# A decoder trunk on one core: four modulation vectors moved from TensorE to VectorE, low halves of the first mixer's weights no longer made ahead, and a planner with other durations

## The chip, the cores and the metric

The kernel runs on one core of a Trainium2 chip. The metric is the device time of one execution in microseconds, as the median of several runs. TensorE (PE) does the matrix products and transposes, VectorE (DVE) and ScalarE (ACT) the elementwise work, GpSimd (POOL) a few small operations. SyncE (SP) issues every transfer, in order, on one queue.

## What is computed

Two layers, each made of a SwiGLU feed-forward block, a token mixer and a second feed-forward block, on 256 tokens of width 1024 in float32. A conditioning vector gives nine modulation vectors per layer: a shift, a scale and a gate for each of the three sub-layers. Cut to what matters here:

```python
cond = silu(c)                                   # 1 x 1024
for l in range(2):
    mod = cond @ ada_w[l] + ada_b[l]             # 9 vectors of 1024
    sh1, sc1, gt1, sh2, sc2, gt2, sh3, sc3, gt3 = split(mod, 9)
    f1 = swiglu(x * (1 + sc1) + sh1, w1, w3, w2)             # F = 2816
    x = layer_norm(2**0.5 * x + 0.5 * gt1 * f1)
    m = token_mixer(x * (1 + sc2) + sh2)         # w_in 1024x2560, w_out 1024x1024
    x = layer_norm(2**0.5 * x + gt2 * m)
    f2 = swiglu(x * (1 + sc3) + sh3, v1, v3, v2)
    x = layer_norm(2**0.5 * x + 0.5 * gt3 * f2)
```

The mixer has three parts side by side: a gated linear recurrence, chunked retention, and a diagonal state-space model ("S5") whose output is `y = Re(C x)`, a complex product taken as sums of real ones.

## The kernel before

**Products in three terms.** Every large product is made from float32 operands split in a high half, rounded to fp32r, and a low half, the rest: three fp32r products for one (`mm3`, tiles `xTh`, `xTl` for the activations, `g_slot` for the hidden units, `wh_slot`, `wl_slot` for the weights). A weight block of 128x2048 (1 MB) arrives in a `raw_slot` (3 of them). ScalarE casts each half of it to `wh_slot`, VectorE subtracts to give `wl_slot` (8 of each, 128x1024). `Piece.convert` (line 805) does that. A block that is needed later can be split ahead: `ahead` and `split_ahead` (lines 844 to 858) load it, make its halves and store only the low halves in DRAM (`gtdl...`). When the block is used, its raw form is loaded again and cast again, and the low halves come by a transfer instead of VectorE's subtraction. Before the change this is done for the four blocks of `mix_w_out` of both layers and for six of the ten blocks of layer 1's `mix_w_in`.

**Modulation vectors, two ways.** `ada_matmul` (line 955) leaves a vector to TensorE: 8 chunks of `ada_w` (128x1024, 512 KB each) in `s_slot` tiles meet the condition repeated over 32 columns (`condrep`), 32 plain float32 products of 32x256 for a vector, in two fused groups of 16. `ada_group` (line 903) leaves four vectors to VectorE and ScalarE: 32 chunks hold rows of all four at once; half of them are multiplied by the condition and added by one VectorE instruction (`SCALAR_TENSOR_TENSOR`), the other half are scaled by ScalarE and added by VectorE (`TENSOR_TENSOR` 128x1024), and at the end TensorE transposes the sum and VectorE reduces it. Before, layer 0's vectors 2 to 7 go the first way and ten others the second. Vectors 0 and 1 have their own start. Vector 2 is the gate of the first sub-layer; 3 and 4 are shift and scale of the first mixer; 5 is its gate.

**Order.** Nothing of the order on the engines is written by hand. The program records all operations (`Scheduler.add`, line 325), each with a duration from `cost` (line 411). A list scheduler (`run`, line 496) lays them out in eight rounds with priorities from the round before (`place_late`), picks buffers as well, and keeps the round with the shortest planned span; `emit` writes the instructions in planned order. So any change of a duration or of the work can move instructions and buffers anywhere. The program text sets only what may stand where: `Background` items (modulation, parameters, low halves made ahead) are recorded between the units of a feed-forward block.

**S5 output.** `y_part` (line 1547) multiplies the scanned states by tables on VectorE, and TensorE sums the result over the states (32-column products with `CT`, four to a fused group). For the first half of the states (`u == 0`) VectorE first adds or subtracts the two products, so that TensorE has two groups; for the second half TensorE takes all four.

Profile lines all read L694, the line of `emit` from which every instruction is issued; instructions are told apart by their tiles.

Of the kernel before, what the change touches and what calls it, by code (L numbers as in the profile page):

```python
# [14 lines left out]
ALU = mybir.AluOpType  # L15
PSUM = bass.MemoryType.PSUM
# [126 lines left out]
class Op:  # L143
    __slots__ = ("i", "eng", "calls", "dur", "deps", "succ", "tiles", "banks", "func", "prio", "start", "end",
                 "alts", "pref", "pdur", "nbytes", "outname")
# [108 lines left out]
class Scheduler:  # L254
# [70 lines left out]
    def add(self, eng, m, real, a, k, alts=()):  # L325
# [21 lines left out]
        fs = 1  # L347
# [14 lines left out]
        for x, w in accs:  # L362
# [38 lines left out]
            self.hist[nm] = keep  # L401
        d, nb = op.dur, op.nbytes
        c = self.cost(eng, m, a, k, out, ins, nel, fs, scal, psum, op)
        if not first and out.shape[0] == 32:
            c = 27
        op.dur, op.nbytes = d + c, nb + op.nbytes
        op.pref, op.pdur = op.eng, op.dur
        for i, n, r in alts:
            op.alts[i] = (r, self.cost(i, n, a, k, out, ins, nel, fs, scal, psum, op))

    def cost(self, eng, m, a, k, out, ins, n, fs, scal, psum, op):
        if eng == E_SPQ:
            nb = 4
            for x in list(out.shape):
                nb *= x
            run = min(nb // (x_runs(out)), nb // x_runs(ins[0]))
            op.nbytes = nb * (0.94 if run >= 4096 else 1) if run >= 512 else max(2 * nb, nb // run * 157)
            src = ins[0].ap_ if isinstance(ins[0], VT) else ins[0]
            return 635 if "DRAM" not in str(src.space) or len(src.shape) != len(out.shape) else 460
        if eng == E_PE:  # L420
            if m == "transpose":
                op.nbytes = fs * ins[0].shape[0] / 128
                return 109.5
            cols = fs
            op.nbytes = fs * (1 if "float32r" in str(ins[0].dtype) else 4) * ins[0].shape[0] / 128
            if "float32r" in str(ins[0].dtype):
                return cols * 0.4246 + 8.6
            return max(cols, 128) * 4 * 0.4167 + 5
# [21 lines left out]
        if m == "tensor_copy":  # L450
            return 100 + 3.4 * n
        ops = str(k.get("op", k.get("op0", "")))
        if "pow" in ops:
            return 1075 + 68 * n
# [41 lines left out]
    def run(self, span, slack):  # L496
# [23 lines left out]
        info = self.tile_info  # L520

# [52 lines left out]
        while done < n:  # L574
# [41 lines left out]
            d = op.dur  # L616
            if op.func is not None and op.func:
                if cur_set is None or op.func not in cur_set:
                    d += 1280
                    cur_set = next(fs for fs in ACT_SETS if op.func in fs)  # L620
# [12 lines left out]
            if e == E_SPQ:  # L633
                efree[e] = s + d
                st = max(dma_free, s + 1060)
                dma_free = st + op.nbytes / 360
                op.end = dma_free + 1000
            else:
                op.end = s + d
                efree[e] = op.end  # L640
            for b in op.banks:
                bank_last.setdefault(b, {})[e] = op.end
# [61 lines left out]
def trunk_kernel(ctx: ExitStack, tc: tile.TileContext, a: dict, cst: bass.AP, out: bass.AP):  # L704
# [715 lines left out]
    def mixer(l, P, nxt, last_features, bg):  # L1420
# [126 lines left out]
        def y_part(u, ch):  # L1547
# [11 lines left out]
            for n, tabs in enumerate(((tcv, tsv), (tsv, tcv))):  # L1559
                p = [t2([128, 4, 128], f"pr{l}{ch}{u}{n}{i}") for i in range(2)]  # L1560
                for i, tab in enumerate(tabs):
                    VG.tensor_tensor(p[i], v[u][i][:, ch], tab[:, js, :], op=ALU.mult)
                    if u:
                        y_mm((0, 1)[i] if n == 0 else 2, p[i], n + i == 0, n + i == 2)
                if u == 0:
                    GV.tensor_tensor(p[0], p[0], p[1], op=ALU.add if n else ALU.subtract)
                    y_mm(2 * n, p[0], n == 0, n == 1)
# [368 lines left out]
    with tc.manual_schedule():  # L1936
# [17 lines left out]
        for l in range(L):  # L1954
            mp = mix_params(l, Ps[l])
            if l == 0:
# [5 lines left out]
                items = adam((0, 2), (0, 3), (0, 4), (0, 5))  # L1962
                extra = dict(enumerate([param_start] + param_steps()))
                extra.update({7: mp[0], 9: mp[1], 10: mp[2], 11: mp[3], 13: mp[4], 14: mp[5]})
                bg = Background(merge(attach(items, extra), ahead(0, [], (0, 256, 512, 768))), 5)
                late = Background(adam((0, 6), (0, 7)), 3)
            else:
                items = ada([(1, 5), (1, 6), (1, 7), (1, 8)])
                bg = Background(merge(attach(items, {2: mp[0], 4: mp[1], 6: mp[2], 8: mp[3], 10: mp[4], 12: mp[5]}),
                                      ahead(1, all_in[4:], (0, 256, 512, 768))), 7)  # L1970
# [35 lines left out]
```

## Time and profile before

| | |
|---|---|
| median of 3 runs | 1055.18 us (1053.9 to 1064.11) |
| profiled execution | 1052.99 us, of it 1051.2 us from first to last instruction |
| granted TensorE clock, mean | 0.99 |
| PE busy | 1007.4 us (96%) |
| PE weight loads busy | 893.4 us (85%) |
| DVE busy | 822.4 us (78%) |
| ACT busy | 572.3 us (54%) |
| moved by DMA | 304.94 MB, mean 290 GB/s |

A busy share is a mean over stages with different limits, so the rows below give it by stage too. Matmuls are pipelined: a row's duration runs past the start of the next one, and what a matmul costs PE is the distance from one start to the next. The feed-forward block of layer 0 runs to about 226 us, its mixer to about 361, the second block to about 533; layer 1 follows with bounds at about 737 and 858.

### The profile page before, as it was taken

How to read it: one execution, taken by the hardware profiler on the slowest of the kernel's cores; microseconds unless marked ns; L12 is line 12 of the kernel's file. 1: busy time of each engine (PE TensorE's matmuls, PEld its weight loads, DVE VectorE, ACT ScalarE, POOL GpSimd, SP SyncE). 2: the span in 40 equal slices, each digit the busy share in tenths (PEclk: the TensorE clock that was granted, in tenths of full speed). 3: DMA queues.
4: the chain of work that ended last, by engine and by line, in shares of the span. 5: the costliest groups of instructions: out<-in, count | busy, mean ns of one | idle time of the engine just before them, and what ended most of it. 6: DMA issues, size and time to landing. Idle time of an engine off the chain costs nothing.

```text
span 1051.2 us, 17641 instructions
## 1 busy us (share of the span) xinstructions
PE 1007.4 (96%) x7061; PEld 893.4 (85%) x7061; DVE 822.4 (78%) x1276; ACT 572.3 (54%) x737; POOL 27.9 (3%) x46
## 2 busy tenths in 40 slices
PE   5999999999988999999999999999999899999996
PEld 3788888888976789999987989999898779999995
DVE  3676675669998999999889999666989788554555
ACT  3565564334478666655547565555447755444440
POOL 0000000000001000000000000000000100000000
PEclk9999999999999999999999999999999999999999
DMA  9999989985679789999967999998478736555521
GB/s 362 404 339 354 355 333 362 378 319 192 216 250 351 252 284 388 400 373 344 355 253 265 337 385 366 355 360 315 163 289 360 301 123 237 176 186 201 188 93 40
DMA packets 70002, 304.94 MB, mean 290 GB/s; under 512 B 15520, under 2 KB 18080, under 8 KB 47904
## 3 DMA queue, kind: packets, MB, share of 16 engines
q1 hardware_dynamic: 69920, 303.82, 78.1%
q8 instruction: 55, 0.90, 0.3%
q14 instruction: 27, 0.22, 0.1%
HBM read 286.46 MB, written 15.75 MB: 287 GB/s over the span
## 4 chain that ended last, share of the span: by engine, by line
PE 79%; DVE 11%; DMA 6%; ACT 1%; issue 1%; SPq 0%; DVEq 0%; ACTq 0%
PE r_slot L694 79%; DVE s_slot L694 5%; DMA raw_slot<-in_pack_dram 5%; DVE wl_slot L694 3%; DVE x_res L694 1%; DMA s_slot<-in_ada_w_dram 1%; DVE ti_slot L694 1%; ACT wh_slot L694 1%; DMA g_slot<-g_slot 1%; SPq L694 0%; DVE xTl L694 0%; ACT s_slot L694 0%; DVE xTh L694 0%; DVE g_slot L694 0%; ACT L694 0%
## 5 line engine op out<-in xcount | busy, mean ns | idle before, releaser
L694 ACT CAST wh_slot<-raw_slot 128x1024 fp32r<-128x1024 f32 x348 | 355.9, 1049 | 274.6 <-PE r_slot L694 128.4
L694 DVE TENSOR_TENSOR wl_slot<-raw_slot,wh_slot 128x1024 fp32r<-128x1024 f32 x320 | 384.0, 1219 | 145.1 <-ACT wh_slot L694 136.7
L694 PE MATMUL r_slot<-xTh,wh_slot 128*128 128x256 f32 x1216 | 341.3, 281 | 0.0
L694 PE MATMUL r_slot<-xTh,wl_slot 128*128 128x256 f32 x1216 | 341.0, 281 | 0.0
L694 PE MATMUL r_slot<-xTl,wh_slot 128*128 128x256 f32 x1216 | 340.5, 280 | 0.0
L694 PEld LDWEIGHTS r_slot<-xTh,wl_slot 128*128 128x128 f32 x1216 | 231.7, 191 | 1.6 <-issue 1.6
L694 PEld LDWEIGHTS r_slot<-xTh,wh_slot 128*128 128x128 f32 x1216 | 229.1, 188 | 2.0 <-issue 0.8
L694 PEld LDWEIGHTS r_slot<-xTl,wh_slot 128*128 128x128 f32 x1216 | 229.0, 188 | 1.2
L694 PE MATMUL r_slot<-wh_slot,g_slot 128*128 128x512 f32 x704 | 224.7, 392 | 0.5 <-DVE g_slot L694 0.5
L694 PEld LDWEIGHTS r_slot<-wh_slot,g_slot 128*128 128x128 f32 x704 | 131.8, 188 | 27.4 <-DVE g_slot L694 0.9
L694 PE MATMUL r_slot<-wh_slot,xTh 128*128 128x512 f32 (+1 forms) x416 | 146.0, 352 | 5.8 <-DVE xTh L694 3.9
L694 PE MATMUL r_slot<-wh_slot,xTl 128*128 128x512 f32 (+1 forms) x416 | 144.0, 349 | 2.7 <-DVE xTl L694 2.7
L694 PE MATMUL r_slot<-wl_slot,xTh 128*128 128x512 f32 (+1 forms) x416 | 143.7, 347 | 0.5 <-DVE wl_slot L694 0.5
L694 PE MATMUL r_slot<-wl_slot,g_slot 128*128 128x512 f32 x352 | 137.5, 391 | 0.0
L694 DVE TENSOR_TENSOR s_slot<-s_slot,s_slot 128x256 f32<-128x256 f32 (+10 forms) x168 | 109.6, 676 | 6.8 <-ACT s_slot L694 4.3
L694 PEld LDWEIGHTS r_slot<-wh_slot,xTh 128*128 128x128 f32 x416 | 79.2, 191 | 18.4 <-DVE xTh L694 5.4
L694 PEld LDWEIGHTS r_slot<-wh_slot,xTl 128*128 128x128 f32 x416 | 79.3, 191 | 17.6 <-DVE xTl L694 4.4
L694 DVE TENSOR_TENSOR s_slot<-r_slot,s_slot 128x512 f32<-128x512 f32 x100 | 67.8, 683 | 28.4 <-PE r_slot L694 28.1
L694 PEld LDWEIGHTS r_slot<-wl_slot,xTh 128*128 128x128 f32 x416 | 79.3, 191 | 10.1 <-DVE wl_slot L694 0.7
L694 PEld LDWEIGHTS r_slot<-wl_slot,g_slot 128*128 128x128 f32 x352 | 66.1, 188 | 12.4 <-issue 0.4
L694 ACT ACTIVATE s_slot<-s_slot,cond 128x1024 f32<-128x1024 f32 x40 | 46.1, 1152 | 36.2 <-DMA s_slot<-in_ada_w_dram 36.1
L694 DVE SCALAR_TENSOR_TENSOR s_slot<-s_slot,cond,s_slot 128x1024 f32<-128x1024 f32 x37 | 47.3, 1278 | 4.5 <-DMA s_slot<-in_ada_w_dram 4.3
(123 smaller groups left out, 685.9 us busy)
## 6 DMA issues: line engine op xcount, KB each, us to landing
raw_slot<-in_pack_dram SPq DMA_DIRECT2D x172, 1024.0 KB
s_slot<-in_ada_w_dram SPq DMA_DIRECT2D x128, 512.0 KB
s_slot<-in_pack_dram SPq DMA_DIRECT2D x16, 512.0 KB
tdlmix_w_out<-wl_slot SPq DMA_DIRECT2D x12, 512.0 KB
wl_slot<-tdlmix_w_out SPq DMA_DIRECT2D x12, 512.0 KB
s_slot<-gtd SPq DMA_DIRECT2D x6, 512.0 KB
s_slot<-in_ln_g_dram SPq DMA_DIRECT2D x6, 512.0 KB
s_slot<-in_ln_b_dram SPq DMA_DIRECT2D x6, 512.0 KB
```

What stands on the lines that cost most here:

```text
L694: real(*[self.place(v) for v in a], **{n: self.place(v) for n, v in k.items()})
```

## The change

Six things are edited. (1) The planner's durations: float32 products of 32 rows cost more, small ones less; GpSimd's copies and powers cost less; a long transfer counts 0.97 of its bytes, not 0.94. (2) A new function `port` marks operations that use the read port shared by VectorE and GpSimd, and the planner lets a GpSimd operation wait for the end of a VectorE operation that is so marked. (3) Layer 0's vectors 2 to 5 go through `ada_group`, one group of four, not four times through `ada_matmul`. (4) No low halves are made ahead for layer 0's `mix_w_out`. (5) For layer 1 the blocks of `mix_w_in` that are split ahead go from six to three; its `mix_w_out` stays as it is. (6) In `y_part` TensorE takes all four products for both halves of the states, and VectorE's additions and subtractions there are gone.

```diff
         d, nb = op.dur, op.nbytes
         c = self.cost(eng, m, a, k, out, ins, nel, fs, scal, psum, op)
         if not first and out.shape[0] == 32:
-            c = 27
+            c = 27 if (len(op.calls) - 1) % 4 else 1.695 * fs
...
+    def port(self, eng, m, out, ins):
+
+        if eng == E_POOL:
+            return 3 if ins else 0
+        if eng != E_DVE:
+            return 0
+        psum = ["PSUM" in str((x.ap_ if isinstance(x, VT) else x).space) for x in [out] + ins]
+        if m in ("tensor_tensor", "tensor_tensor_scan", "scalar_tensor_tensor"):
+            return 0 if psum[1] or psum[-1] else 1
+        return 1 if m in ("tensor_scalar", "tensor_copy") and not psum[0] and not psum[1] else 0
...
-            op.nbytes = nb * (0.94 if run >= 4096 else 1) if run >= 512 else max(2 * nb, nb // run * 157)
+            op.nbytes = nb * (0.97 if run >= 4096 else 1) if run >= 512 else max(2 * nb, nb // run * 157)
...
-            return max(cols, 128) * 4 * 0.4167 + 5
+            return max(cols, 64) * 4 * 0.4167 + (65 if out.shape[0] == 32 else 5)
...
         if "pow" in ops:
-            return 1075 + 68 * n
+            return 394 + 156 * n
...
+            if op.port == 3 and s < held:
+                d = held - s + d - 140
...
+                if e == E_DVE and op.port:
+                    held = op.end
...
-                    if u:
-                        y_mm((0, 1)[i] if n == 0 else 2, p[i], n + i == 0, n + i == 2)
-                if u == 0:
-                    GV.tensor_tensor(p[0], p[0], p[1], op=ALU.add if n else ALU.subtract)
-                    y_mm(2 * n, p[0], n == 0, n == 1)
+                    y_mm((0, 1)[i] if n == 0 else 2, p[i], n + i == 0, n + i == 2)
...
-                items = adam((0, 2), (0, 3), (0, 4), (0, 5))
+                items = ada([(0, 2), (0, 3), (0, 4), (0, 5)])
...
-                bg = Background(merge(attach(items, extra), ahead(0, [], (0, 256, 512, 768))), 5)
+                bg = Background(merge(attach(items, extra), ahead(0, [], ())), 5)
...
-                                      ahead(1, all_in[4:], (0, 256, 512, 768))), 7)
+                                      ahead(1, all_in[7:], (0, 256, 512, 768))), 7)
```

In the built programs TensorE loses 128 of its 192 `condrep` products of 32x256 and gains 32 of `CT`. VectorE gains 15 `SCALAR_TENSOR_TENSOR` and 16 `TENSOR_TENSOR` of 128x1024, one `TENSOR_SCALAR` and two reductions, and loses eight `TENSOR_TENSOR` of 128x512; its count of low halves stays at 320. ScalarE loses 14 casts of weights and 4 copies and gains 16 scalings. SP loses 7 loads of raw blocks, 14 stores and 14 loads of low halves.

TensorE, in the first feed-forward block of layer 0, before: one fused group of a modulation vector (`condrep`, each row four products) between products of the up and down weights.

```order
L694 MATMUL r_slot_131<-wl_slot_80,g_slot_102 128x512
L694 MATMUL r_slot_124<-s_slot_92,condrep 32x256 x4
L694 MATMUL r_slot_124<-s_slot_93,condrep 32x256 x4
L694 MATMUL r_slot_124<-s_slot_83,condrep 32x256 x4
L694 MATMUL r_slot_124<-s_slot_84,condrep 32x256 x4
L694 MATMUL r_slot_126<-xTh,wl_slot_76 128x256
L694 MATMUL r_slot_131<-wh_slot_73,g_slot_103 128x512
```

VectorE, in the same block, of the change: the same vectors as multiply-adds on `cond` and additions of 128x1024, between low halves (`wl_slot`) and parameter work (`ssmq`).

```order
L712 SCALAR_TENSOR_TENSOR s_slot_85<-s_slot_89,cond_135,s_slot_85 128x1024
L712 TENSOR_TENSOR ssmq<-ssmq,ti_slot_122 128x16
L712 TENSOR_TENSOR ssmq<-ssmq,ti_slot_116 128x16
L712 TENSOR_TENSOR wl_slot_81<-raw_slot_64,wh_slot_73 128x1024
L712 TENSOR_TENSOR ssmq<-ssmq,ti_slot_116 128x16
L712 TENSOR_TENSOR s_slot_86<-s_slot_93,ssmq 128x128 x3
L712 TENSOR_TENSOR s_slot_86<-s_slot_86 64x8x16 x2
L712 TENSOR_TENSOR s_slot_86<-s_slot_93,ssmq 128x128
L712 TENSOR_TENSOR s_slot_87<-s_slot_87,s_slot_82 128x1024
```

Eight such groups of 16 products have left TensorE in this block, and 16 pairs of such VectorE rows have come.

TensorE, at the end of that block, before: the transposes of the first 128 tokens (`cs,x_res`) for the mixer, with the down products (`wh_slot,g_slot`) of the other 128 tokens around them.

```order
L694 MATMUL r_slot_127<-wh_slot_71,g_slot_104 128x512
L694 MATMUL r_slot_127<-wl_slot_79,g_slot_104 128x512
L694 MATMUL r_slot_125<-cs,x_res 128x128 x4
L694 MATMUL r_slot_127<-wh_slot_71,g_slot_106 128x512
L694 MATMUL r_slot_129<-cs,x_res 128x128 x4
L694 MATMUL r_slot_124<-cs,modFM 32x128
L694 MATMUL r_slot_128<-cs,s_slot_99 128x128 x2
```

The same place of the change, the first rows behind the transposes.

```order
L712 MATMUL r_slot_126<-cs,x_res 128x128 x4
L712 MATMUL r_slot_130<-cs,x_res 128x128 x4
L712 MATMUL r_slot_127<-wh_slot_70,g_slot_105 128x512
L712 MATMUL r_slot_127<-wl_slot_78,g_slot_105 128x512
L712 MATMUL r_slot_127<-wh_slot_70,g_slot_107 128x512
L712 MATMUL r_slot_127<-wh_slot_71,g_slot_105 128x512
L712 MATMUL r_slot_127<-wl_slot_79,g_slot_105 128x512
```

Before, one down product stands behind the first transposes; of the change 18 do, seen until the mixer's first `xTh` product. From the transposes that open layer 0's mixer to those that close it there are 26 more 128x512 products in all (18 of the down weights where there was 1, 9 more of the output weights), and 21 more in layer 1's mixer (11 and 10).

VectorE, at the end of layer 0's mixer, before: low halves of the output weights came from DRAM here, and two multiply-adds of the second block's modulation (`cond`) stand among the norm of the retention part (`gn`) and the low halves of the activations (`xTl`).

```order
L694 SCALAR_TENSOR_TENSOR s_slot_88<-s_slot_86,cond_134,s_slot_88 128x1024
L694 TENSOR_TENSOR xTl<-s_slot_100,xTh 128x2x128
L694 SCALAR_TENSOR_TENSOR s_slot_88<-s_slot_85,cond_134,s_slot_88 128x1024
L694 TENSOR_TENSOR wl_slot_74<-raw_slot_64,wh_slot_68 128x1024
L694 TENSOR_TENSOR xTl<-r_slot_124,xTh 128x3x128
L694 TENSOR_TENSOR xTl<-s_slot_100,xTh 128x2x128
```

The same place of the change.

```order
L712 TENSOR_TENSOR s_slot_99<-s_slot_99,gn 128x384
L712 TENSOR_TENSOR wl_slot_80<-raw_slot_65,wh_slot_72 128x1024
L712 TENSOR_TENSOR s_slot_99<-s_slot_99,s_slot_98 128x384
L712 TENSOR_TENSOR wl_slot_81<-raw_slot_65,wh_slot_73 128x1024
L712 TENSOR_TENSOR wl_slot_76<-raw_slot_63,wh_slot_68 128x1024
L712 TENSOR_TENSOR xTl<-r_slot_131,xTh 128x3x128
```

Counted on VectorE from the last statistics (`BN_AGGR`) of the first block to the first of the mixer, there are 17 low halves before and 24 of the change; three multiply-adds, three 128x1024 additions and four 128x512 additions that stood there before do not any more. From the mixer's last statistics to the second block's first, where there were 27 multiply-adds there are 29, and one 128x1024 addition more; low halves stay at 64. In layer 1's mixer the low halves go from 7 to 10.

## Rows read from the trace of the kernel before

**Rows 1.** Page, busy time, share of the span, instructions.

```profile
PE 1007.4 (96%) x7061; PEld 893.4 (85%) x7061; DVE 822.4 (78%) x1276; ACT 572.3 (54%) x737; POOL 27.9 (3%) x46
```

**Rows 2.** Busy time by stage; PEclk is the granted clock, DMA its busy share.

```profile
core 0: us, PE busy (x) PEld busy (x) DVE busy (x) ACT busy (x) POOL busy (x), PEclk, DMA share, GB/s
0.00:226.00 226.00, 214.60 (x1558) 176.11 (x1559) 136.49 (x261) 113.41 (x161) 4.58 (x18) 0.99 0.96 363
226.00:241.00 15.00, 14.05 (x98) 10.95 (x96) 14.83 (x29) 8.55 (x13) 0.67 (x2) 1.00 0.70 258
241.00:353.00 112.00, 100.87 (x792) 88.64 (x793) 106.50 (x206) 69.44 (x95) 6.60 (x5) 0.98 0.71 255
353.00:361.00 8.00, 5.73 (x28) 4.34 (x27) 7.81 (x17) 6.91 (x8) 0.56 (x1) 1.00 0.79 272
361.00:533.00 172.00, 172.00 (x1186) 159.86 (x1187) 162.21 (x178) 103.00 (x120) 2.26 (x5) 0.99 0.92 345
...
553.00:737.00 184.00, 181.80 (x1235) 167.62 (x1236) 153.55 (x197) 108.88 (x132) 2.72 (x4) 0.99 0.93 340
737.00:757.00 20.00, 18.27 (x117) 15.80 (x115) 19.79 (x38) 11.65 (x20) 2.01 (x2) 1.00 0.41 143
757.00:848.00 91.00, 87.32 (x692) 78.33 (x693) 78.87 (x169) 55.03 (x79) 3.19 (x4) 0.98 0.76 290
848.00:870.00 22.00, 21.05 (x99) 16.78 (x98) 20.71 (x39) 13.44 (x20) 2.03 (x2) 1.00 0.54 188
```

**Rows 3.** Chain that ended last, in order of time: start, us, what.

```profile
16.66 209.46 PE r_slot L694 x1530
...
297.06 10.10 DVE s_slot L694 x18
...
360.88 171.96 PE r_slot L694 x1184
```

**Rows 4.** TensorE in order of time, first block of layer 0: start, duration, instruction.

```profile
118.18 1.93 PE L694 MATMUL r_slot<-s_slot,condrep 128*32 128x256 f32 x32
120.04 0.38 PE L694 MATMUL r_slot<-xTh,wl_slot 128*128 128x256 f32 x1
```

**Rows 5.** The same, the end of that block.

```profile
222.45 0.39 PE L694 MATMUL r_slot<-wl_slot,g_slot 128*128 128x512 f32 x1
222.68 0.39 PE L694 MATMUL r_slot<-wh_slot,g_slot 128*128 128x512 f32 x1
222.90 0.39 PE L694 MATMUL r_slot<-wl_slot,g_slot 128*128 128x512 f32 x1
```

**Rows 6.** Groups by form, VectorE: form, count, busy us, mean ns, idle before.

```profile
L694 DVE TENSOR_TENSOR wl_slot<-raw_slot,wh_slot 128x1024 fp32r<-128x1024 f32 x320 | 384.0, 1219 | 145.1 <-ACT wh_slot L694 136.7 <-PE r_slot L694 4.9 <-issue 2.0
...
L694 DVE TENSOR_TENSOR s_slot<-s_slot,s_slot 128x1024 f32<-128x1024 f32 x40 | 48.7, 1217 | 3.3 <-ACT s_slot L694 3.3
L694 DVE SCALAR_TENSOR_TENSOR s_slot<-s_slot,cond,s_slot 128x1024 f32<-128x1024 f32 x37 | 47.3, 1278 | 4.5 <-DMA s_slot<-in_ada_w_dram 4.3
L694 DVE TENSOR_TENSOR s_slot<-s_slot,s_slot 128x512 f32<-128x512 f32 x46 | 29.6, 681 | 3.4 <-PE r_slot L694 1.9 <-ACT s_slot L694 1.1
```

**Rows 7.** Busy time, layer 1's first block, its first 60 us.

```profile
553.00:613.00 60.00, 57.94 (x359) 51.19 (x359) 56.74 (x72) 38.91 (x50) 2.61 (x3) 1.00 0.88 321
```

**Rows 8.** TensorE in order of time, in layer 1's mixer.

```profile
816.67 0.43 PE L694 MATMUL r_slot<-s_slot,CT 128*32 128x128 f32 x8
817.02 0.39 PE L694 MATMUL r_slot<-wh_slot,xTl 128*128 128x256 f32 x1
```

**Rows 9.** Page, DMA issues: tiles, count, size of each.

```profile
raw_slot<-in_pack_dram SPq DMA_DIRECT2D x172, 1024.0 KB
...
tdlmix_w_out<-wl_slot SPq DMA_DIRECT2D x12, 512.0 KB
```

**Rows 10.** Busy time in 25 us of the last block.

```profile
900.00:925.00 25.00, 25.00 (x192) 24.06 (x191) 12.32 (x12) 11.06 (x12) 0.00 (x0) 1.00 0.54 179
```

## What is expected of the change

> **What bounds the kernel now.** I read the page first: PE is busy 1007.4 of 1051.2 us and DVE 822.4 [rows 1]. A mean over stages does not say who sets the time, so I then read the busy time by stage [rows 2]. Three kinds of stage show. In the second feed-forward block of layer 0 (361 to 533) PE is busy without a gap, 172.0 of 172.0, and in layer 1's first block 181.8 of 184.0. In the first block of layer 0 (0 to 226) it is busy 214.6, and the chain has one piece of 209.46 us and 1530 TensorE instructions from 16.66 us on, in which nothing is waited for [rows 3]. Only the mixers differ: from 226 to 361 DVE is busy 14.8 + 106.5 + 7.8 = 129.1 of 135 us while PE has 0.9 + 11.1 + 2.3 = 14.3 us idle, and the chain there has pieces such as 10.10 us of 18 VectorE operations [rows 2, 3]. In layer 1's mixer (737 to 870) DVE is busy 119.4 of 133 and PE idles 6.4 us [rows 2]. So PE sets the time in the blocks and DVE in layer 0's mixer; layer 1's mixer lies between.
>
> What a matmul costs PE is read from starts, not from durations: 128x512 products show 0.39 us but start 0.23 us apart [rows 5].
>
> **Vectors 2 to 5 off TensorE.** A fused group of 16 products (32 records) starts at 118.18 us, and the next product at 120.04: 1.86 us of PE [rows 4]. Eight groups go, all in the first block: 8 x 1.86 = **-14.9 us**, because PE is never waited out there. The least gain is nothing, should another engine be the bound there (a rival below).
>
> What comes on DVE: 15 multiply-adds at 47.3/37 = 1.28 us, 16 additions at 48.7/40 = 1.22 us [rows 6], and a scaling and two reductions that I price at no more than a multiply-add each. That is 19.2 + 19.5 + at most 3.8, some 41 us. The eight low halves that are no longer made ahead in this block give back 8 x 384.0/320 = 9.6 us [rows 6]. DVE goes from 136.5 to about 168 us, in a stage that shrinks to about 211: 80% [rows 2]. ACT is busy 113.4 of 226 [rows 2] and gains 16 scalings against 8 casts, so it has room. The cover is DVE's 89 us of idle time; without it every added instruction stands ahead of a low half or a gate product in DVE's queue, and 38.7 us would show. The nearest row for the price is layer 1's first block between 553 and 613, where a group of four vectors is worked the same way with DVE at 56.7 of 60 us: PE loses 60 - 57.9 = 2.1 us [rows 7]. I take **+2.1 us**, between 0 and 38.7.
>
> Transfers: at 363 GB/s the first 226 us move 82.0 MB [rows 2]. Four raw blocks of 1.05 MB and eight stores of 0.52 MB go [rows 9], 8.4 MB; the chunks of the vectors stay. 73.6 MB need 203 us at the same rate, less than PE's 211, so DMA stays covered, by less than 10 us. The gate, vector 2, now comes with the other three, and its trip through DRAM stands four transfers ahead of its reload in SP's order. Raw blocks wait behind that reload; I leave it at nothing, since three `raw_slot` blocks lie ahead, and count a few us in the range.
>
> **Layer 0's mixer.** Eight low halves of the output weights are now subtracted where they are used. Between the statistics that bound the mixer on DVE the order shows 7 more low halves, but 3 multiply-adds, 3 large and 4 small additions fewer: 7 x 1.20 - 3 x 1.28 - 3 x 1.22 - 4 x 29.6/46 = 8.4 - 3.8 - 3.7 - 2.6 = -1.7 us [rows 6]. At the two ends of the stretch a low half, an addition and a scaling more stand, at most 3 us. DVE's load, which sets this stretch, thus grows by **+1 us**. PE meanwhile has 26 more 128x512 products here, which came out of the neighbouring blocks, and covers them with idle time: 26 x 0.23 = 6.0 of 14.3 us [rows 2, 5]. The blocks shorten by that: **-6.0 us** (0 to -6.0). The four extra `CT` groups take 817.02 - 816.67 = 0.35 us each, 1.4 us, also under DVE [rows 8].
>
> **Second block of layer 0.** The multiply-adds put off by the mixer land here: 2 multiply-adds and one addition more, 3.8 us on a DVE that is busy 162.2 of 172 [rows 2, 6]. That is 97%, and a wait of PE can come: **+1 us** (0 to 3.8).
>
> **Layer 1.** Its first block loses three raw loads, six casts and six stores, all beside a full PE: 0. Its mixer has 7 more low halves with its ends (8.4 us) and 4 additions fewer (2.6 us), so DVE comes to 119.4 + 5.8 = 125 of 133 us. PE gains 1.4 us for `CT` and 21 moved products, 4.8 us, of which the 6.4 us of idle time should take a part. The blocks lose 4.8; I let the mixer lose 3.4 of it again, and the `CT` groups count: **0 us** (-4.8 to +7).
>
> **The planner's durations** cost nothing themselves; what they do is the order, and it is counted above.
>
> Sum, against the profiled execution: 1053.0 - 14.9 + 2.1 + 1 - 6.0 + 1 + 0 = 1036.2 us. That execution lies 2.2 us below the median of the runs shown, so a median may lie 0 to 2 us above the sum: **1037 us**.
>
> **A rule that speaks against it.** In the first block weight loads are busy 176.1 of 226 us, 78%, while in a stretch of the last block they are busy 24.06 of 25, 96%; PE's own row shows a full engine in both [rows 2, 10]. The Trainium skill, "Perfetto Trace Analysis", section "Identifying the Most-Contended Engine", says that matmul busy time is no good measure of TensorE's headroom and that weight-load busy time (with MFU) is. By that rule TensorE has about a fifth to spare in the first block, and less work there would bring nothing: 1049 us, the third rival. By the row of the chain (1530 instructions, no wait) the whole 14.9 count. I follow the row: a `condrep` group and the 128x512 products hold PE longer for each weight load than the 128x256 products do, so the lower share need not be room.
>
> **Rivals.**
>
> 1. *Slower.* The 31 added VectorE instructions in the first block stand in DVE's order between low halves, and PE waits for the low half behind each. In full: 1053.0 - 16.8 - 2.1 + 38.7 = 1073 us; slower than before as soon as more than 19 of the 38.7 us reach PE. For it: the order alternates them. Against it: DVE idles 89 us there, eight `wl_slot` buffers lie ahead of PE, and the stretch 553 to 613 lost 2.1 us under a heavier load [rows 2, 7].
> 2. *The mixers give it back.* The 14 low halves, 16.8 us, less the 8 additions, 5.1 us, lengthen both mixers in full, and nothing is moved into their idle time: 1053.0 - 14.9 + 2.1 + 11.7 = 1052 us. For it: DVE is at 96% in layer 0's mixer. Against it: the order shows the load there net unchanged.
> 3. *The first block does not shorten.* Its DMA share is 0.96 [rows 2]; weights or DVE, not PE, set its length, and PE's freed time becomes waiting: 1053.0 - 6.0 + 1 + 1 = 1049 us. Against it: the chain has no DMA piece between 16.66 and 226 us, and the bytes fall too.
> 4. *More than forecast.* The new order also fills half of what idle time the mixers have left, 14.3 - 6.0 + 6.4 = 14.7 us: about 1037 - 7 = 1030 us.
>
> **Chances.** Forecast 0.58, rival 1 0.05, rival 2 0.12, rival 3 0.12, rival 4 0.13. The forecast alone ranges over 1031 to 1045. To leave out no more than 2 in 10, the range reaches from 1028, near the end of rival 4, to rival 2's 1052. One per cent, about what a measurement of this kernel can tell from no change, is 10.6 us from the median, at 1044.6 and 1065.7. Faster: most of the forecast and rival 4, 0.68. Within: the forecast's upper end, rivals 2 and 3, 0.27. Slower: rival 1, 0.05.
>
> **What would show it.** Right: the first block's last PE product some 15 to 19 us earlier, still in one PE piece of the chain; DVE near 80% there; 226 to 361 about as long as before, with PE idle near 8 us; the second block still without a PE gap; about 22 MB less moved (7 raw blocks, 28 transfers of low halves). Wrong: PE waiting for `wl_slot` or for DMA in the first block (rivals 1, 3); a mixer longer by more than 5 us (rival 2); PE gaps in 361 to 533, where DVE has 6 us left; or a granted clock at half speed in more places than the mixers, since PE drops to 1.2 GHz there now and then (0.98 on average in both [rows 2]).

## The result, and the profile after

The changed kernel takes 1040.38 us (median of 4 runs, 1038.88 to 1041.56) against 1054.54 us of the kernel before beside it (4 runs, 1053.83 to 1064.11). The ratio is 0.983, with a 95% interval of 0.980 to 0.987: faster by 1.7%. A second set of runs gave 0.984 (0.979 to 0.989). The prediction was 1037 us with a range of 1028 to 1052. The profiled execution after took 1041.53 us, its span 1039.8.

| | before | after |
|---|---|---|
| PE busy | 1007.4 us (96%) | 995.7 us (96%) |
| DVE busy | 822.4 us (78%) | 851.6 us (82%) |
| moved by DMA | 304.94 MB | 282.91 MB |

The page's line that answers to [rows 1]:

```profile
PE 995.7 (96%) x6869; PEld 889.5 (86%) x6869; DVE 851.6 (82%) x1302; ACT 572.7 (55%) x734; POOL 29.4 (3%) x46
```

To compare stages that have moved, I bound them by something that both traces show: the start on TensorE of the first transposes of the residual stream (`cs,x_res`) for each sub-layer. That gives six stages: first block, mixer and second block of layer 0, then the same of layer 1. The last runs to 1048 and to 1036 here; to the end of VectorE's last instruction, which the table further down takes, it is 195.3 and 195.6 us. Busy time by stage, before (window, its length, PE, PEld, DVE, ACT, POOL, granted clock, DMA share, GB/s):

```profile
0.00:234.36 234.36, 222.96 (x1595) 182.91 (x1596) 144.68 (x277) 116.59 (x165) 5.13 (x19) 0.99 0.95 359
234.36:357.95 123.59, 111.51 (x873) 96.59 (x872) 118.05 (x226) 79.71 (x110) 7.27 (x7) 0.99 0.72 256
357.95:549.75 191.80, 189.04 (x1261) 173.22 (x1261) 180.76 (x216) 112.25 (x131) 3.72 (x6) 0.99 0.89 335
549.75:743.06 193.31, 190.42 (x1277) 174.35 (x1275) 162.69 (x219) 113.70 (x138) 3.27 (x5) 0.99 0.91 332
743.06:852.88 109.82, 104.41 (x804) 93.05 (x803) 96.89 (x202) 66.89 (x100) 5.20 (x6) 0.98 0.70 266
852.88:1048.00 195.12, 189.08 (x1258) 173.25 (x1256) 119.14 (x141) 83.20 (x98) 3.33 (x3) 1.00 0.46 160
```

The same six stages after:

```profile
0.00:216.71 216.71, 204.33 (x1325) 174.49 (x1326) 165.63 (x299) 121.86 (x166) 6.02 (x19) 0.99 0.94 352
216.71:341.50 124.79, 116.16 (x916) 99.76 (x915) 119.69 (x228) 75.89 (x108) 8.94 (x7) 0.99 0.50 185
341.50:531.73 190.23, 187.25 (x1260) 171.47 (x1259) 184.66 (x221) 115.05 (x132) 2.81 (x6) 1.00 0.95 351
531.73:729.13 197.40, 190.38 (x1273) 174.17 (x1272) 158.58 (x211) 110.56 (x136) 3.27 (x5) 0.99 0.83 299
729.13:841.07 111.94, 107.34 (x838) 95.13 (x837) 102.17 (x205) 65.10 (x98) 5.45 (x6) 0.98 0.63 233
841.07:1036.00 194.93, 190.23 (x1266) 174.45 (x1264) 120.18 (x142) 84.26 (x99) 2.95 (x3) 1.00 0.46 160
```

Layer 0 is shorter by 17.65 - 1.20 + 1.57 = 18.0 us, nearly all of it in its first block. Layer 1 is longer by 4.1 + 2.1 + 0.3 = 6.5 us, most of it in its first block, where PE's busy time is the same (190.4 both) and its idle time went from 2.9 to 7.0 us. The chain of waits after shows both (start, us, what):

```profile
17.54 199.12 PE r_slot L712 x1295
...
645.94 8.02 DMA raw_slot<-in_pack_dram
...
656.37 5.93 DMA tdlmix_w_out<-wl_slot
...
663.68 7.65 DMA raw_slot<-in_pack_dram
...
674.88 8.94 DMA raw_slot<-in_pack_dram
683.90 2.00 ACT wh_slot L712 x2
687.14 1.21 DVE sm_slot L712 x2
688.83 40.37 PE r_slot L712 x258
```

The first line answers to the first of [rows 3]: one PE piece from 17.5 us on, now to 216.7. The rest has no counterpart before, where the chain has one PE piece at that place:

```profile
613.14 122.08 PE r_slot L694 x867
```

After, the chain there goes through loads, low halves and the sums of four modulation vectors (`sm_slot`) until 688.83, and PE stands for 3.02 us before the transposes of a gate (`cs,modFM`):

```profile
688.83 0.28 PE L712 MATMUL r_slot<-cs,modFM 128*32 128x128 f32 x1 [3.02 <-DVE modFM L712]
```

### The profile page after: what moved, and what is told of

Its sections match the earlier page's. It is cut to its first block, busy times and chain, and to the rows that moved or that the text cites. A ratio compares the mean times of both kernels' runs of the same rounds, so it can differ in the third digit from the quotient of the medians.

```text
span 1039.8 us, 17216 instructions
## 1 busy us (share of the span) xinstructions
PE 995.7 (96%) x6869; PEld 889.5 (86%) x6869; DVE 851.6 (82%) x1302; ACT 572.7 (55%) x734; POOL 29.4 (3%) x46
## 2 busy tenths in 40 slices
DMA packets 64962, 282.91 MB, mean 272 GB/s; under 512 B 14960, under 2 KB 17520, under 8 KB 43760
## 4 chain that ended last, share of the span: by engine, by line
PE 62%; DVE 21%; DMA 10%; issue 3%; ACT 3%; SPq 1%; POOL 0%; DVEq 0%; ACTq 0%
PE r_slot L712 62%; DVE wl_slot L712 8%; DVE s_slot L712 8%; DMA raw_slot<-in_pack_dram 6%; DMA s_slot<-in_ada_w_dram 2%; DVE x_res L712 2%; ACT wh_slot L712 1%; DMA g_slot<-g_slot 1%; DVE xTl L712 1%; DVE ti_slot L712 1%; SPq L712 1%; ACT s_slot L712 1%; DMA tdlmix_w_out<-wl_slot 1%; DVE g_slot L712 1%; ACT L712 0%
## 5 line engine op out<-in xcount | busy, mean ns | idle before, releaser
L712 ACT CAST wh_slot<-raw_slot 128x1024 fp32r<-128x1024 f32 x334 | 343.5, 1050 | 277.7 <-PE r_slot L712 148.5
L712 DVE TENSOR_TENSOR s_slot<-s_slot,s_slot 128x1024 f32<-128x1024 f32 (+10 forms) x176 | 123.9, 725 | 6.2 <-PE r_slot L712 3.7
L712 PEld LDWEIGHTS r_slot<-wl_slot,xTh 128*128 128x128 f32 x416 | 79.5, 191 | 14.7 <-DVE wl_slot L712 2.6
L712 ACT ACTIVATE s_slot<-s_slot,cond 128x1024 f32<-128x1024 f32 x56 | 64.5, 1152 | 40.8 <-DMA s_slot<-in_ada_w_dram 40.8
L712 DVE SCALAR_TENSOR_TENSOR s_slot<-s_slot,cond,s_slot 128x1024 f32<-128x1024 f32 x52 | 67.2, 1292 | 2.7 <-DMA s_slot<-in_ada_w_dram 2.7
```

Of the source, the lines that this page charges most:

```text
L712: real(*[self.place(v) for v in a], **{n: self.place(v) for n, v in k.items()})
```

## The experiments

Each experiment is the changed kernel with one edit, timed against the kernel before on the same chip. The unused statistics, none ahead and the two other orders ran on another chip than the rest, so ratios are compared and not times. "Above" is the difference of its ratio from the 0.9841 of the changed kernel's second set, times 1057 us. The last column forms the product of time and mean granted clock for every run, means it for the experiment and for its runs of the kernel before, and shows the difference; for the changed kernel that is -16.4. It is an estimate of what would be left at equal clock, and a rough one: two orders of the same work give -16.8 and -11.2.

| run | median us (before beside it) | ratio and 95% interval | above, us | time x clock, against before |
|---|---|---|---|---|
| changed, again | 1040.85 (1058.45) | 0.984, 0.979 to 0.989 | 0 | -16.4 |
| vectors back on TensorE | 1052.92 (1056.74) | 0.996, 0.994 to 0.999 | +12.8 | -2.3 |
| unused products added | 1062.71 (1056.74) | 1.004, 1.001 to 1.008 | +21.4 | +4.0 |
| unused statistics added | 1044.42 (1057.58) | 0.987, 0.984 to 0.990 | +3.2 | -14.7 |
| layer 0's low halves ahead | 1057.07 (1058.45) | 0.999, 0.996 to 1.001 | +15.3 | -7.1 |
| six blocks ahead, layer 1 | 1047.69 (1058.45) | 0.991, 0.987 to 0.994 | +7.0 | -12.4 |
| none ahead, layer 1 | 1044.16 (1057.58) | 0.987, 0.984 to 0.991 | +3.4 | -13.1 |
| sums on VectorE | 1051.49 (1058.45) | 0.995, 0.992 to 0.998 | +11.8 | -10.4 |
| old durations, new work | 1048.81 (1056.74) | 0.991, 0.988 to 0.994 | +7.4 | -10.7 |
| new durations, old work | 1060.46 (1056.74) | 1.004, 1.000 to 1.007 | +20.5 | +1.1 |
| other order, a | 1043.55 (1057.58) | 0.986, 0.980 to 0.992 | +2.1 | -16.8 |
| other order, b | 1043.76 (1057.58) | 0.987, 0.984 to 0.990 | +3.2 | -11.2 |

Lengths of the six stages in each profiled execution, bounded as above:

| run | block | mixer | block | block | mixer | block |
|---|---|---|---|---|---|---|
| before | 234.4 | 123.6 | 191.8 | 193.3 | 109.8 | 195.3 |
| changed | 216.7 | 124.8 | 190.2 | 197.4 | 111.9 | 195.6 |
| changed, again | 214.1 | 127.3 | 188.5 | 197.7 | 111.9 | 195.6 |
| vectors back on TensorE | 232.7 | 124.9 | 188.8 | 192.1 | 112.0 | 195.6 |
| unused products added | 233.0 | 128.3 | 194.7 | 197.2 | 111.9 | 195.6 |
| unused statistics added | 217.5 | 128.5 | 193.9 | 192.4 | 113.5 | 195.6 |
| layer 0's low halves ahead | 232.9 | 125.7 | 192.0 | 198.2 | 108.6 | 195.1 |
| six blocks ahead, layer 1 | 217.1 | 129.8 | 191.1 | 200.2 | 110.1 | 195.6 |
| none ahead, layer 1 | 218.4 | 125.5 | 194.2 | 190.1 | 118.7 | 195.7 |
| sums on VectorE | 217.8 | 127.1 | 195.3 | 200.5 | 112.5 | 195.4 |
| old durations, new work | 222.0 | 120.5 | 199.3 | 198.7 | 107.7 | 195.1 |
| new durations, old work | 233.0 | 127.8 | 196.5 | 199.7 | 111.5 | 195.6 |
| other order, a | 216.2 | 127.5 | 193.8 | 202.5 | 107.3 | 195.4 |
| other order, b | 214.8 | 124.9 | 190.5 | 200.3 | 110.5 | 195.6 |

The changed kernel again, as the reference of the second set:

> The changed kernel itself, run beside the three that follow, so that they can be held against it on the same chip. Expected: 0.98 to 0.987 of the kernel before, as in its first runs.

It came out as expected.

### Is TensorE the bound of the first block?

One part undone:

```diff
-                items = ada([(0, 2), (0, 3), (0, 4), (0, 5)])
+                items = adam((0, 2), (0, 3), (0, 4), (0, 5))
```

> The changed kernel with one part undone: vectors 2 to 5 of layer 0 are made by 4-column-group products on TensorE again (8 fused groups), all else as changed. Theory (TensorE is the bound of layer 0's first block, 198.9 us of its own work in 216.7 us): the 8 groups put 8 x 1.86 = 14.9 us back on TensorE and take about 20 us from VectorE, which was no bound there; first block 230 to 235 us, total 1052 to 1056 us. Rival (the block is set by VectorE or by the loads, and the new durations alone made the plan better): the block stays within 3 us of 216.7, total 1037 to 1044 us.

And the removed products alone put back, with nothing taken from VectorE; the kernel's own results are as before:

```diff
+                def idle_products(i):
+                    ps = bank(f"idle{i}")
+                    for j in range(1):
+                        with sch.fused():
+                            for kk in range(4):
+                                for b_ in range(4):
+                                    PE.matmul(ps[32 * b_:32 * b_ + 32, 0:256], condrep[:, kk, :],
+                                              x_res[:, 0, 256 * b_:256 * b_ + 256], start=(kk == 0), stop=(kk == 3))
+                    S.copy(tiny([128, 4], f"idlec{i}"), ps[:, 0:4])
+                items = attach(items, {2 * i: (lambda i=i: idle_products(i)) for i in range(8)})
```

> The changed kernel, to which 8 fused groups of 16 products of the removed form (fp32, 32 columns wide, in four column groups) are added in layer 0's first block; they read the residual stream and the conditioning weights already loaded, need no further load or VectorE work, and what they give is not used. VectorE keeps the vectors. Theory (TensorE bound): each group costs its full 1.86 us, first block +13 to +17 us, total 1053 to 1058 us. Rival (VectorE's new 20 us, or the loads, bound the block now): TensorE has 17.8 us of stall there to take them in, first block +0 to +4 us, total 1040 to 1045 us.

Both first blocks are 16.0 and 16.3 us longer than the changed kernel's first profile, 18.6 and 18.9 longer than its second. The groups' own time is 8 x 1.86 = 14.9 us. Added products that need no load and no VectorE work (only a small copy on ScalarE for each group) thus cost their full time: TensorE is the bound. The rival is out. Busy time of the whole block, first of the vectors back on TensorE, then of the unused products:

```profile
0.00:232.73 232.73, 220.70 (x1581) 181.20 (x1582) 131.85 (x265) 107.66 (x156) 5.13 (x19) 0.99 0.88 328
```

```profile
0.00:233.02 233.02, 218.86 (x1580) 180.05 (x1581) 168.57 (x299) 122.03 (x174) 6.15 (x19) 0.99 0.89 327
```

VectorE has 131.85 us of work in one and 168.57 in the other, and the length is the same. PE's count agrees (1581 and 1580 rows), and the bytes, 232.73 us x 328 GB/s = 76.3 MB and 233.02 x 327 = 76.2, are those of the changed kernel, 216.71 x 352 = 76.3. The unused products cost 21 us in all, more than the block and more than either forecast. The second block of layer 0, untouched by the edit, is 4.5 us longer in that profile than in the changed kernel's; what orders alone do is shown further down.

### Was taking the low halves out of that block free?

```diff
-                bg = Background(merge(attach(items, extra), ahead(0, [], ())), 5)
+                bg = Background(merge(attach(items, extra), ahead(0, [], (0, 256, 512, 768))), 5)
```

> The changed kernel with one part undone: the low halves of layer 0's output weights are made ahead again, in its first block (4 raw blocks more to load, 8 halves to store and to load again), and the mixer has 8 subtractions fewer. Theory (the planner had filled the mixer's idle time of TensorE with other products and the extra subtractions cost it about 1 us net): within 4 us of the changed kernel, with 12.6 MB more moved. Rival 2 of the prediction (the subtractions lengthen the mixer in full, 8 x 1.2 = 9.6 us): 8 to 11 us faster than the changed kernel, the stretch of layer 0's mixer 127 us, not 137. A third way (the added transfers bind the first block, which is now 18 us shorter): first block +4 to +10 us.

The block grew as in the third way, and by more than that way had: the first block is 232.9 us long, as long as with the eight product groups back, though TensorE's work is that of the changed kernel. PE, and then ACT, between 60 and 231 us in this run (line, what it waited for: us, times, longest):

```profile
PE r_slot L712 <- ACT wh_slot L712: 4.9, 4, 1.6
PE r_slot L712 <- DVE wl_slot L712: 4.1, 4, 1.8
```

```profile
ACT wh_slot L712 <- DMA raw_slot<-in_pack_dram: 22.5, 11, 3.9
```

The same wait of ACT in the changed kernel, from 60 to 216 us, and in the kernel before, from 60 to 231:

```profile
ACT wh_slot L712 <- DMA raw_slot<-in_pack_dram: 1.4, 1, 1.4
```

```profile
ACT wh_slot L694 <- DMA raw_slot<-in_pack_dram: 17.2, 8, 6.2
```

So TensorE waits 9.0 us for halves. That ScalarE waits for raw blocks does not by itself make them late: before, it waits for them nearly as long, and TensorE never. TensorE's waits lie between 119 and 171 us. Busy time around them, with the low halves ahead and in the changed kernel:

```profile
110.00:171.00 61.00, 52.00 (x313) 45.31 (x311) 59.99 (x125) 37.91 (x56) 1.27 (x3) 0.92 0.96 375
```

```profile
110.00:171.00 61.00, 61.00 (x437) 56.98 (x436) 60.87 (x120) 41.61 (x59) 2.23 (x4) 1.00 0.97 359
```

In the changed kernel three things are full here at once: TensorE, VectorE (60.87 of 61 us) and nearly the loads (a DMA share of 0.97). The edit adds to the last two. The block moves 232.88 us x 355 GB/s = 82.7 MB instead of 76.3, and VectorE has eight subtractions more, 8 x 1.2 = 9.6 us. The chain of waits between 60 and 231 us goes through raw loads for 18.9% and through low halves on VectorE for 15.7%. Which of the two makes the halves late is not shown, since the edit brings both. The granted clock, 0.92 here, adds to the loss.

A rate does not settle it. Before, the block moved 234.36 us x 359 GB/s = 84.1 MB, but that rate is no ceiling, as a stretch of the same block shows:

```profile
20.00:30.00 10.00, 10.00 (x57) 6.91 (x55) 5.68 (x11) 5.67 (x9) 0.31 (x1) 1.00 1.03 408
```

The Trainium skill, "Perfetto Trace Analysis", section "Engine Utilization", gives 358 GB/s as a core's share when both cores of a pair use the memory, and says that a core alone can pull more. The row's 408 agrees.

What is shown is how the two edits act together. With the vectors on TensorE the first block takes 233.0 us with the low halves ahead (the run with new durations and the old work) and 232.7 without. With the vectors on VectorE it takes 232.9 with them and 216.7 or 214.1 without; in the five other runs with that work and the new durations it takes 214.8 to 218.4, so an order alone does not make the 16 us. Each edit alone is worth next to nothing, and together they are worth the 17.7 us.

### Is VectorE's idle time there usable?

```diff
+                def idle_stats(i):
+                    for j in range(2):
+                        V.bn_stats(tiny([128, 6], f"idles{i}{j}"), x_res[:, 0, 512 * j:512 * j + 512])
+                items = attach(items, {i: (lambda i=i: idle_stats(i)) for i in range(1, 15)})
```

> The changed kernel, to which 28 statistics of 128x512 (0.69 us each, 19.3 us in all) are added on VectorE in layer 0's first block; they read the residual stream, need no load, and their results are not used. The prediction let the 41 us of new VectorE work there cost 2.1 us, since VectorE idles in the block. Theory (the 51 us that VectorE still idles there of 217 are usable cover): first block +0 to +3 us, total 1040 to 1044 us. Rival (the idle time lies at the block's ends, and between 60 and 180 us, where VectorE is busy 113.6 of 120 us, each added us reaches TensorE): first block +10 to +19 us, total 1050 to 1060 us.

The first block takes 217.5 us, 0.8 or 3.4 more than in the two profiles of the changed kernel, and the whole +3.2. Between 60 and 180 us, with the statistics and without:

```profile
60.00:180.00 120.00, 118.44 (x808) 108.43 (x807) 118.90 (x212) 81.63 (x109) 3.08 (x7) 1.00 0.98 364
```

```profile
60.00:180.00 120.00, 120.00 (x822) 110.78 (x821) 113.62 (x205) 81.04 (x108) 3.05 (x7) 1.00 0.97 363
```

VectorE goes to 118.9 of 120 us and PE loses 1.6. The planner put 17 of the 28 statistics before 60 us, the others between 62 and 96, and none into the stretch from 96 to 200. The cover was real, but it lies early in the block: the run does not show that VectorE has any between 110 and 171 us.

### Layer 1: blocks split ahead, and what an order alone is worth

Six blocks ahead, as before, and none:

```diff
-                                      ahead(1, all_in[7:], (0, 256, 512, 768))), 7)
+                                      ahead(1, all_in[4:], (0, 256, 512, 768))), 7)
```

> The changed kernel with one part undone: six and not three blocks of layer 1's mixer input weights are split ahead again, in layer 1's first block (3 raw loads, 6 casts, 6 stores, 6 loads more there and in the mixer; 6 subtractions move from the mixer to the block). Theory (all of it lay beside a full TensorE in the block, and the mixer has room for most of it): within 3 us of the changed kernel; the mixer's stretch (126.4 us) shorter by 0 to 3, the block's wait (7.3 us of 183) the same or longer by 0 to 3. Rival (the 6 subtractions are on the path of layer 1's mixer, which grew by 4.8 us): 4 to 7 us faster, the stretch back near 121.6 us.

```diff
-                                      ahead(1, all_in[7:], (0, 256, 512, 768))), 7)
+                                      ahead(1, all_in[10:], (0, 256, 512, 768))), 7)
```

> The changed kernel, with none of layer 1's mixer input blocks split ahead (three before in it, six in the run with that part undone): 3 raw loads, 6 stores and 6 loads of low halves fewer, and 6 more subtractions in layer 1's mixer. If the transfers made ahead are what makes TensorE wait in layer 1's first block (12.0 us of stall with six blocks ahead, 8 with three), the block's stall falls to 4 or less. The mixer's VectorE (88 of 97.7 us) takes 7.2 us more: by the step of the prediction that put that under cover the stretch grows by 2 us or less and the total is 1036 to 1041 us; if VectorE sets it, by 6 to 8 us, and the total is 1042 to 1047 us.

And two orders of the same work:

```diff
-                return cols * 0.4246 + 8.6
+                return cols * 0.4250 + 8.6
```

> The changed kernel, work unchanged; one duration of the planner differs by a thousandth (0.4250 for 0.4246 ns a column of an fp32r product), which gives another order from layer 0's first block on, with a planned span shorter by 1.3 us. It shows what an order alone is worth. Theory (the parts undone one at a time cost 7 to 16 us because their work and transfers cost that): within 4 us of the changed kernel, 1036 to 1045 us. Rival (the order of the changed kernel is a lucky one, and any other order costs 5 us or more): 1045 to 1052 us.

```diff
-SETTINGS = [(7900, 5800)]
+SETTINGS = [(6000, 5000)]
```

> The changed kernel, work unchanged, other limits for the planner's late placing (6000 and 5000 for 7900 and 5800 ns), which keeps the order of layer 0's first block and gives another from layer 0's mixer on, with a planned span of 0.2 us less. Theory: within 4 us of the changed kernel, the first block within 2 us of it. Rival (a lucky order): 1045 to 1052 us, with the loss behind the first block.

With six, three and none ahead, layer 1's first block takes 200.2, 197.4 to 197.7 and 190.1 us, and its mixer 110.1, 111.9 and 118.7. Six ahead came out 7.0 us slower, which neither of its forecasts had. Without any ahead, the chain of waits has one long PE piece in that block again:

```profile
619.16 81.03 PE r_slot L712 x593
```

PE idles 0.8 us in the block then, against 7.0 in the changed kernel, and the mixer does pay for subtractions, 6.8 us for 6 x 1.2 = 7.2. Total +3.4, within the second of the two forecasts. The other orders set the caution: the same work takes 202.5 and 200.3 us in that block, and 192.1 and 192.4 in two of the runs above. The step from six to three is inside that spread and is not shown. The step to none is outside it, but by 2 us and in one profile, so that the loads and stores made ahead make TensorE wait there is likely and not shown. Order a has 1036.19 us in its fastest run and 1048.88 in its slowest, order b 1041.42 to 1044.70; both medians are 2 to 3 us above the changed kernel. By its median neither order costs the 5 us that the rival asked for, though order a's interval reaches 0.992, 8 us above. A difference of 3 us between two plans can't be put down to their work.

### The sums on VectorE

```diff
-                    y_mm((0, 1)[i] if n == 0 else 2, p[i], n + i == 0, n + i == 2)
+                    if u:
+                        y_mm((0, 1)[i] if n == 0 else 2, p[i], n + i == 0, n + i == 2)
+                if u == 0:
+                    GV.tensor_tensor(p[0], p[0], p[1], op=ALU.add if n else ALU.subtract)
+                    y_mm(2 * n, p[0], n == 0, n == 1)
```

> The changed kernel with one part undone: the sums of the first half of the states are formed on VectorE again (8 additions of 128x512, 5.4 us over both layers, back on VectorE; 8 groups of 4 products, 8 x 0.35 = 2.8 us, off TensorE). Theory (VectorE sets layer 0's mixer, neither sets layer 1's alone): slower by 0 to 4 us. Rival (TensorE's added products were the dearer part, as both mixers have TensorE above 94% by now): faster by 1 to 3 us.

Slower by 11.8 us, beyond both theories. The two mixers, where this work stands, are 127.1 and 112.5 us, as in the changed kernel (124.8 to 127.3 and 111.9): the sums themselves cost nothing that can be seen. The loss stands in the two blocks behind layer 0's mixer (195.3 and 200.5 us), which have none of the sums. In the first of them PE waits once for a gate:

```profile
PE r_slot L712 <- DVE modFM L712: 3.7, 1, 3.7
```

The same wait stands in the two runs with unused work, 2.75 and 2.80 us, where that block takes 194.7 and 193.9 us, so it can come without the sums. At equal clock 6 of the 11.8 us are left, about what two orders of the same work can differ by. That another order made the loss is likely; it was not tested further.

### The planner's durations

The planner part of one kernel was joined with the work of the other.

> The work of the changed kernel, planned with the durations of the kernel before. Theory (the moved work makes the gain, the durations only shuffle the order): within 4 us of the changed kernel, 1037 to 1045 us. Rival (the measured durations make the gain): 1048 to 1055 us.

> The work of the kernel before, planned with the new durations and the shared-port rule. Theory: within 4 us of the kernel before, 1050 to 1058 us. Rival (the measured durations make the gain): 1038 to 1044 us.

The new durations cost 0.35% with the old work (interval 0.0 to 0.7%) and save 7.4 us with the new. With the old ones both mixers are shorter (120.5 and 107.7 us), and the first block and the one behind the mixer are longer (222.0 and 199.3). Neither theory came out: 1048.81 us lies in the rival's 1048 to 1055, and 1060.46 above 1050 to 1058. Durations alone did not make the gain, since the rival asked for 1038 to 1044 with the old work; but of the 16.8 us that the changed kernel gains, the moved work alone makes 9.4, and 7.4 need the new durations with it.

## Why the prediction was right

**What bounds the kernel.** Right for the first block, by the two runs that put the products back. Incomplete in one point: [rows 2] showed a DMA share of 0.96 there, and I took it for a bound that lies just behind TensorE. The chain shows one engine only. With TensorE's work lowered alone the block keeps its length, so another limit, loads or VectorE, was level with it.

**-14.9 for the vectors.** Right in size, 16.0 to 18.9 us measured, and only together with the edit that I had priced at nothing. The third rival's mechanism was true of the kernel with that edit left out. My sum escaped it because it was made for both edits. I had counted the bytes that leave as room, 8.4 MB against 84.1 - 76.3 = 7.8 measured; whether it was the bytes or the eight subtractions that had to leave is open.

**+2.1 for VectorE.** Right that it is small. With 17 products of 0.23 us moved out, the block's terms make -14.9 + 2.1 - 3.9 = -16.7 against -17.7. DVE is busy 165.6 of 216.7 us, 76%, where the text said near 80. Between 110 and 171 us it is busy 60.87 of 61.00, so the 89 us of cover that I counted were spread unevenly.

**Layer 0's mixer, +1.** 123.6 to 124.8 us (127.3 in the changed kernel's second profile), with DVE's work up by 1.6 and PE's idle time down from 12.1 to 8.6 (forecast near 8). Rival 2 is out: with the low halves made ahead again, the mixer is not 9.6 us shorter but within 2.

**Second block, +1.** With 9 products of 0.23 us moved out the forecast is 1 - 2.1 = -1.1. It is shorter by 1.6, with no gap of PE beyond its 3.0 us idle (2.8 before), at a DVE load of 97% as forecast.

**Layer 1, 0.** The step that failed: +6.5 us, at the upper end of the range given (+7). I reasoned that loads and casts which leave lie beside a full TensorE, and looked at amounts. What decides is when the four vectors' sum is ready: the transposes of a gate stand in PE's order and wait 3.02 us for it, behind a string of loads. Before, the chain has no such wait. That block has the same work in seven of the runs (the two profiles of the changed kernel, the vectors back, both with unused work, both orders) and takes 192.1 to 202.5 us. Of the two short ones, 192.1 has no wait of 0.25 us or more for that gate and 192.4 one of 1.64; the five long ones, 197.2 to 202.5, wait 2.93 to 5.67 us for it, and the granted clock falls there. So the order sets it, by this wait first; why one order has the sum ready in time is open.

**The sum.** 1036.2 against 1041.5 in the profile, 1040.4 in the median. Layer 0 gave -18.0 for -16.8, layer 1 +6.5 for 0.

**The planner's durations, nothing by themselves.** That holds for the old work (0.35% slower). With the new work they carry 7.4 us, which the sum took in only as the order that I read.

**The rule on weight loads.** The Trainium skill, "Perfetto Trace Analysis", section "Identifying the Most-Contended Engine", takes weight-load busy time, with MFU, as the measure of TensorE's headroom. MFU was not worked out here. By the weight loads' share TensorE would be a fifth free in this block, and the unused products free of charge; they cost 16 us or more. The weight loads' share does not tell the cases apart: 180.05 of 233.02 us (77%) where TensorE is the bound, 177.18 of 232.88 (76%) where it waits for halves. The row of the latter:

```profile
0.00:232.88 232.88, 211.57 (x1326) 177.18 (x1327) 176.52 (x307) 128.29 (x174) 5.16 (x19) 0.97 0.94 355
```

My reason for following the chain was wrong for the `condrep` groups. Their 32 weight loads in 1.86 us are 0.06 us each, less than the 0.12 of a 128x256 product. What lowers the share is that these loads run side by side. The weight loads of the 12 groups before, to 226 us, are busy 11.3 us out of 12 x 1.86 = 22.3, though 384 of 111 ns one after another would take 42.6:

```profile
L694 PEld LDWEIGHTS r_slot<-s_slot,condrep 128*32 128x32 f32 x384 | 11.3, 111 | 12.8 <-issue 6.1 <-DVE condrep L694 0.7 <-ACT s_slot L694 0.4
```

None of the variants has a lower ratio than the changed kernel.

## What to carry to other kernels

Where the chain shows one engine without a wait, still work out how full every other resource is, in stretches of that stage: a mean over the stage (VectorE 76%) can hide one that is full (60.87 of 61 us), and a mean rate is no ceiling (359 GB/s, with 408 in one stretch). If two are level, an edit on one can be worth nothing until the other falls, and an ablation of one part will show the whole gain for each. Before a few us are put down to a part of a planned kernel, time two other orders of the same work.

## What was not expected of the hardware

A wait of TensorE can cost more than its length, because the granted clock can fall behind it. After the 3.02 us wait for the gate, in 1-us windows of the changed kernel:

```profile
687.00:688.00 1.00, 0.00 (x0) 0.00 (x0) 1.00 (x3) 0.00 (x0) 0.00 (x0) 1.00 1.03 434
688.00:689.00 1.00, 0.17 (x2) 0.18 (x3) 0.74 (x5) 0.21 (x1) 0.00 (x0) 1.00 0.77 324
689.00:690.00 1.00, 1.00 (x10) 1.00 (x10) 0.02 (x1) 1.00 (x2) 0.00 (x0) 0.87 0.11 45
690.00:691.00 1.00, 1.00 (x6) 1.00 (x6) 1.00 (x1) 0.95 (x2) 0.00 (x0) 0.50 0.06 25
```

PE is busy again from 689, but at 0.50, 1.2 GHz. Its products of 128x256 start 0.21 us apart there, 0.12 before the wait:

```profile
684.58 0.28 PE L712 MATMUL r_slot<-xTl,wh_slot 128*128 128x256 f32 x1
684.70 0.28 PE L712 MATMUL r_slot<-xTh,wl_slot 128*128 128x256 f32 x1
...
691.28 0.41 PE L712 MATMUL r_slot<-xTh,wh_slot 128*128 128x256 f32 x1
691.49 0.41 PE L712 MATMUL r_slot<-xTl,wh_slot 128*128 128x256 f32 x1
```

Much of the spread between runs of one program goes with it: the four runs of other order a took 1036.19 to 1048.88 us at mean clocks of 0.993 to 0.980, and their products lie between 1027.9 and 1029.7. It is not all: over the ten runs with new durations and the old work the products range from 1041.4 to 1050.1. It also enlarges what an edit with more waits costs: making layer 0's low halves ahead costs 15.3 us by the clock on the wall and, by the estimate in the table, 9.3 at equal granted clock (from -16.4 to -7.1).
